# A gated encoder block on one core: four dense units in seven quarter products, results through DRAM, the gMLP output branch beside the last head

## The chip, the cores and the metric

One core of a Trainium2 chip runs the whole kernel in one launch. Its engines work side by side, each through its own list of instructions in order: TensorE (PE, matrix products into the accumulators of PSUM), VectorE (DVE), ScalarE (ACT), GpSimd (POOL) and SyncE (SP, which only issues DMAs here). DMAs are issued by SP and POOL. The metric is the device time of one execution in microseconds (us), the median of the runs shown. The profile is of one further execution of the same program.

## What is computed

One block with batch 1, 1024 tokens and width 1024, cut to what matters here:

```python
h = rmsnorm(x, norm_g) * (1 + scale(c)) + shift(c)
q, k, v, z_gla, ra_f, ra_b, u, vs, z_gmlp, m_gla, m_gmlp = split(h @ w_in)
# GLA: 4 heads, two directions, chunks of 64 tokens, then a norm per head
y_gla  = (norm(gla_fw(q, k, v, ra_f) + gla_bw(q, k, v, ra_b)) * silu(z_gla)) @ w_br_gla
# gMLP: chunks of 128 tokens, 8 groups of 128 features
vs     = layernorm(gelu(vs)) * ln_g + ln_b
sg     = einsum('gts,bnsgc->bntgc', gmlp_ws, vs) + gmlp_bs
y_gmlp = (gelu(u) * sg * silu(z_gmlp)) @ w_br_gmlp
merged = sigmoid(m_gla) * y_gla + sigmoid(m_gmlp) * y_gmlp
out    = rmsnorm(x + gate(c) * (merged @ w_out), final_g)
```

u, z_gmlp, m_gla and m_gmlp are four products of the same h (1024 x 1024) with a 1024 x 1024 weight each. They are the "dense units that share activations".

## The kernel before, in words

**Operands.** Every large product is made of three matmuls. An operand is split into a high part (ACT rounds it to fp32r: `split_w`, L123) and a low part (DVE subtracts: L124), and the product is high x high, high x low, low x high (L140 to L142). h is kept as `H_hi` and `H_lo`, eight tiles each of [128 features, 1024 tokens], in 16 slots of pool `hp`. A weight block of 128 output features is [128, 1024], 512 KB, loaded by SP into `ws` (L117), split into `wh` and `wl`.

**`dense_fm`** (L133) makes one block of 128 output features over all tokens: for each half of the tokens it accumulates 8 chunks x 3 matmuls of 512 columns in one accumulator (three of these, tag `d`, rotate) and hands it to an `evac` function.

**Order of the work.** The startup builds h and with it the first column half of vs; then the second half (`evac_vs1`, L393), each tile followed by `ln` (L382: gelu, statistics, scaling, and a pass each for the gain `lng` and the bias `lnb`), the spatial products (L399 to L408, `sg` kept in SBUF), then stage M2 (L420 to L443): eight times a block of u and a block of z_gmlp, and their product split into `gg_hi`, `gg_lo`. Stage M3 (L446 to L485) builds the residual gate (eight loads `wg`, L459, sums on DVE, two matmuls) and takes eight times a block of m_gmlp, tanh, and a block of the gMLP output branch (`FB_YB`), whose result goes to DRAM as `y2_d` (L482, issued by POOL). Then GLA: `dense_q`, `dense_v0`, `dense_k`, `dense_z` for head 0; in the loop over heads (L774) the dense blocks of head h+1 stand beside the chain of head h (`front`, `body`), which is given a high priority; beside heads 2 and 3 stand the eight blocks of m_gla (`dense_ma`, L740). A head's result goes to `g_d` in DRAM (L736). At the end all heads' results are loaded and split (L792 to L803), the GLA output branch (`ev_ya`, L818) merges both branches, and the projection with `w_out` (L883 to L899) ends with the residual and the final norm.

**Who sets the order.** The instructions are written as a program; a planner then orders each engine's list. It takes what is ready by its own estimate of time, earlier written lines first, unless a priority, `keep_in_program_order` or `issue_after` says otherwise. A tile waits for the last use of the slot that it takes. A pool that is opened where another lay waits tile by tile for what lies under it.

Of the kernel before, what the change touches and what calls it, by code (L numbers as in the profile page):

```python
# [37 lines left out]
PC_C, PC_NG, PC_BA, PC_GN = 0, 8, 16, 32  # L38
# packed rows
PR_FG, PR_LG, PR_LB, PR_BG, PR_BS, PR_C = 0, 1, 2, 3, 4, 5  # L40
# [3 lines left out]
def hybrid_block_kernel(ctx: ExitStack, tc: tile.TileContext, x, wf, wt, wada, wgate, wvr, wst, alpha, abias,  # L44
# [18 lines left out]
    cw, wp = pool("wp")  # L63
    dr = ctx.enter_context(tc.tile_pool(name="dr", bufs=1, space=DRAM))
    y2_d = dr.tile([KC, P, T], F32, tag="y2d", name="y2_d")
    g_d = dr.tile([KC - 2, P, T], F32, tag="gd", name="g_d")
# [32 lines left out]
    pcol = cp.tile([P, 40], F32, name="pcol")  # L99
    RT = cp.tile([P, T], F32R, name="RT")  # L100
# [6 lines left out]
    H_hi = [None] * KC  # L107
    H_lo = [None] * KC
    for k in range(KC):
        H_hi[k] = hp.tile([P, T], F32R, tag="h", bufs=16, name=f"hhi{k}")  # L110
        H_lo[k] = hp.tile([P, T], F32R, tag="h", bufs=16, name=f"hlo{k}")

    pin = [True]

    def stage(src):
        w = wp.tile([P, 1024], F32, tag="ws", bufs=2, name=nm("ws"))
# [8 lines left out]

    def fm_weights(b):
        w = stage(wf[b])
        hi = wp.tile([P, KC, P], F32R, tag="wh", bufs=2, name=nm("wh"))
        lo = wp.tile([P, KC, P], F32R, tag="wl", bufs=2, name=nm("wl"))
        split_w(w, hi.rearrange("p k c -> p (k c)"), lo.rearrange("p k c -> p (k c)"))  # L130
        return hi, lo

    def dense_fm(b, xh, xl, evac):  # L133
        """out^T block b (128 features) over all tokens; evac(half, psum)"""
        hi, lo = fm_weights(b)
        for half in range(2):
            acc = pd()
            sl = slice(half * 512, half * 512 + 512)
            for k in range(KC):
                TE.matmul(acc, lhsT=hi[:, k, :], rhs=xh[k][:, sl], start=(k == 0), stop=False)  # L140
                TE.matmul(acc, lhsT=hi[:, k, :], rhs=xl[k][:, sl], start=False, stop=False)  # L141
                TE.matmul(acc, lhsT=lo[:, k, :], rhs=xh[k][:, sl], start=False, stop=(k == KC - 1))  # L142
            evac(half, acc)

    def tm_weights(w0, p_, tag, bufs, prep=None):
        pieces = []
        for j in range(4):
# [3 lines left out]
            hi = p_.tile([P, 2, 512], F32R, tag=tag, bufs=bufs, name=nm("th"))  # L151
            lo = p_.tile([P, 2, 512], F32R, tag=tag, bufs=bufs, name=nm("tl"))
            split_w(w, hi.rearrange("p k c -> p (k c)"), lo.rearrange("p k c -> p (k c)"))
# [3 lines left out]
    def tm_step(acc, pieces, xh, xl, k, t):  # L157
        hi, lo = pieces[k // 2]
        tsl = slice(t * P, t * P + P)
        TE.matmul(acc, lhsT=xh[k][:, tsl], rhs=hi[:, k % 2, :], start=(k == 0), stop=False)  # L160
        TE.matmul(acc, lhsT=xh[k][:, tsl], rhs=lo[:, k % 2, :], start=False, stop=False)  # L161
        return TE.matmul(acc, lhsT=xl[k][:, tsl], rhs=hi[:, k % 2, :], start=False, stop=(k == KC - 1))  # L162

    def dense_tm(pieces, xh, xl, evac, tokens=range(NT)):
        for t in tokens:
            acc = pd()
            for k in range(KC):
# [802 lines left out]
```

## Time and profile before

| | us |
|---|---|
| median of 3 runs | 1119.02 |
| lowest, highest | 1118.24, 1119.49 |
| span of the profiled execution | 1115.8 |
| PE busy in it | 1093.1 |
| DVE, ACT, POOL busy | 567.9, 425.9, 109.7 |

The span runs from the first to the last instruction; the profiled execution has no other time of its own, and what lies around the span (launch and end) is only in the runs' times. A line of the profile's groups gives line, engine and operation, result and operands by the program's names, shapes, count, then busy time in us and mean ns of one, then the engine's idle time just before them and what ended it. The windows view gives, for each stretch of time, its length, PE's busy time with the count of matmuls, the granted clock and the DMA's share and rate. In the timeline a row begins with its start and its duration in us.

### The profile page before, as it was taken

The numbers are of one execution on the slowest core, as the hardware profiler recorded it, in microseconds if no ns is written. First come the engines' busy times: TensorE is split into PE (matmuls) and PEld (weight loads), VectorE is DVE, ScalarE is ACT, GpSimd is POOL, SyncE is SP. The second block draws the span as 40 slices with busy tenths as digits, with TensorE's granted clock in tenths as the row PEclk, the third lists the DMA queues.
The fourth block names the chain that finished last, engine by engine and source line by source line (L and its number), as shares of the span: only waits on it lengthen the run. The fifth ranks groups of instructions, "written<-read, shape, count | busy, mean of one in ns | idle before, by whom it ended". The sixth has DMA issues, their size and how long they took to land.

```text
span 1115.8 us, 13854 instructions
## 1 busy us (share of the span) xinstructions
PE 1093.1 (98%) x5584; PEld 932.1 (84%) x5584; DVE 567.9 (51%) x982; ACT 425.9 (38%) x768; POOL 109.7 (10%) x136
## 2 busy tenths in 40 slices
PE   6899999999999999999999999999999999999996
PEld 4788888888888888889898898899888888888885
DVE  6868753333344111111456787786677534555232
ACT  4452112222221111112565776777576424222232
POOL 3320100000010000000000010000000013013520
PEclk9999999999999999999999999999999999999999
DMA  8632011111153121211020030020111135213412
GB/s 315 251 125 71 1 39 38 57 39 56 54 171 127 64 76 66 82 66 57 22 75 19 22 111 19 20 95 20 58 38 57 38 108 194 76 58 124 160 76 95
DMA packets 25650, 90.39 MB, mean 81 GB/s; under 512 B 3471, under 2 KB 3471, under 8 KB 25586
## 3 DMA queue, kind: packets, MB, share of 16 engines
q1 hardware_dynamic: 18866, 67.27, 17.2%
q0 software_dynamic: 6720, 22.23, 5.8%
q8 instruction: 44, 0.72, 0.3%
q14 instruction: 20, 0.16, 0.0%
HBM read 77.96 MB, written 11.53 MB: 80 GB/s over the span
## 4 chain that ended last, share of the span: by engine, by line
PE 94%; DVE 2%; DMA 1%; ACT 1%; issue 1%; POOL 0%; SPq 0%; POOLq 0%; ACTq 0%
PE pd L140 21%; PE pd L142 21%; PE pd L141 21%; PE pd L161 4%; PE pd L162 4%; PE pd L160 4%; PE pd L765 2%; PE pd L764 2%; PE pd L763 2%; PE pm L404 1%; PE pm L604 1%; PE po L630 1%; PE po L628 1%; PE po L629 1%; PE pd L546 1%; PE pd L547 1%
## 5 line engine op out<-in xcount | busy, mean ns | idle before, releaser
L140 PE MATMUL pd<-hhi,wh 128*128 128x512 f32 x768 | 300.4, 391 | 0.0
L142 PE MATMUL pd<-hhi,wl 128*128 128x512 f32 x768 | 300.4, 391 | 0.0
L141 PE MATMUL pd<-hlo,wh 128*128 128x512 f32 x768 | 300.4, 391 | 0.0
L142 PEld LDWEIGHTS pd<-hhi,wl 128*128 128x128 f32 x768 | 144.3, 188 | 28.9 <-issue 0.2
L140 PEld LDWEIGHTS pd<-hhi,wh 128*128 128x128 f32 x768 | 144.3, 188 | 28.5 <-issue 0.2
L141 PEld LDWEIGHTS pd<-hlo,wh 128*128 128x128 f32 x768 | 144.3, 188 | 28.0
L124 DVE TENSOR_TENSOR wl<-ws,wh 128x1024 fp32r<-128x1024 f32 x64 | 78.1, 1222 | 149.5 <-ACT wh L123 139.4
L123 ACT CAST wh<-ws 128x1024 fp32r<-128x1024 f32 x64 | 67.3, 1051 | 221.2 <-PE pd L141 209.2
L176 POOL TENSOR_TENSOR r<-ms,nhalf 128x1 f32<-128x1 f32 (+1 forms) x24 | 20.6, 859 | 427.9 <-DVE ms L175 422.5
L765 PE MATMUL pd<-tvh,hlo 128*128 128x256 f32 x192 | 54.5, 284 | 0.0
L764 PE MATMUL pd<-tvl,hhi 128*128 128x256 f32 x192 | 54.4, 283 | 0.0
L763 PE MATMUL pd<-tvh,hhi 128*128 128x256 f32 x192 | 54.3, 284 | 0.0
L141 PE MATMUL pd<-ggl,wh 128*128 128x512 f32 x128 | 49.8, 389 | 0.0
L142 PE MATMUL pd<-ggh,wl 128*128 128x512 f32 x128 | 49.8, 389 | 0.0
L141 PE MATMUL pd<-gl,wh 128*128 128x512 f32 x128 | 49.8, 389 | 0.0
L140 PE MATMUL pd<-ggh,wh 128*128 128x512 f32 x128 | 49.8, 389 | 0.0
L142 PE MATMUL pd<-gh,wl 128*128 128x512 f32 x128 | 49.6, 389 | 0.0
L140 PE MATMUL pd<-gh,wh 128*128 128x512 f32 x128 | 48.8, 390 | 0.0
L161 PE MATMUL pd<-tl,mh 128*128 128x512 f32 x120 | 46.8, 390 | 0.4 <-DVE tl L124 0.4
L162 PE MATMUL pd<-th,ml 128*128 128x512 f32 x120 | 46.7, 389 | 0.0
L160 PE MATMUL pd<-th,mh 128*128 128x512 f32 x120 | 45.6, 389 | 0.0
L160 PE MATMUL pd<-th,hhi 128*128 128x512 f32 x104 | 41.6, 404 | 1.2 <-ACT hhi L276 1.2
(246 smaller groups left out, 1986.9 us busy)
## 6 DMA issues: line engine op xcount, KB each, us to landing
ws<-in_wf SPq DMA_DIRECT2D x64, 512.0 KB, 3.5
ws<-in_wt SPq DMA_DIRECT2D x22, 512.0 KB, 3.7
wa<-in_wada SPq DMA_DIRECT2D x16, 512.0 KB, 4.7
xn<-in_x SPq DMA_DIRECT2D x8, 512.0 KB, 5.5
wg<-in_wgate POOLq DMA_DIRECT2D x8, 512.0 KB, 4.2
y_d<-m POOLq DMA_DIRECT2D x16, 256.0 KB, 2.3
y<-y_d POOLq DMA_DIRECT2D x16, 256.0 KB, 4.6
res<-in_x SPq DMA_DIRECT2D x8, 512.0 KB, 6.4
```

Source lines behind the costliest of these rows:

```text
L123: S.copy(hi, w)
L124: V.tensor_tensor(out=lo, in0=w, in1=hi.bitcast(F32), op=ALU.subtract)
L140: TE.matmul(acc, lhsT=hi[:, k, :], rhs=xh[k][:, sl], start=(k == 0), stop=False)
L141: TE.matmul(acc, lhsT=hi[:, k, :], rhs=xl[k][:, sl], start=False, stop=False)
L142: TE.matmul(acc, lhsT=lo[:, k, :], rhs=xh[k][:, sl], start=False, stop=(k == KC - 1))
L160: TE.matmul(acc, lhsT=xh[k][:, tsl], rhs=hi[:, k % 2, :], start=(k == 0), stop=False)
L161: TE.matmul(acc, lhsT=xh[k][:, tsl], rhs=lo[:, k % 2, :], start=False, stop=False)
L162: return TE.matmul(acc, lhsT=xl[k][:, tsl], rhs=hi[:, k % 2, :], start=False, stop=(k == KC - 1))
L176: G.tensor_tensor(out=r, in0=ms, in1=nhalf[:, 0:n], op=ALU.pow)
L763: TE.matmul(o, lhsT=H_hi[k][:, tsl], rhs=hi, start=(k == 0), stop=False)
L764: TE.matmul(o, lhsT=H_hi[k][:, tsl], rhs=lo, start=False, stop=False)
L765: TE.matmul(o, lhsT=H_lo[k][:, tsl], rhs=hi, start=False, stop=(k == KC - 1))
```

## The change

**Seven products.** h and a pair of weight blocks are taken as 2 x 2 quarters: h by feature half and token half (B11, B12, B21, B22), the pair by block and feature half. Instead of eight quarter products (four results, two each), seven are formed, of sums and differences of the quarters (Strassen's scheme in Winograd's form). T1 to T4 are such sums of h, made once on POOL, split, and kept for all sixteen pairs; the sums of the weights are made on POOL for each pair. Three accumulators X, Y, Z are used, with parts in between added by DVE.

**Memory.** h is now tiles of [128, two chunks, 512 tokens] (`Act`), one pool of 30 slots (`ht`) holds h, the sums, x, vs and later all of GLA's tiles. h's quarter B12 is not needed by the products, is written to DRAM (`b12_d`) and read back after the pairs.

**Through DRAM.** `sg`, the gated product `gg`, tanh of m_gla (`ta`) and of m_gmlp (`tb`) are written to DRAM and read where they are used.

**Order.** vs takes tiles 4 to 7, then their spatial products, then tiles 0 to 3 and theirs; the layernorm's gain and bias are applied behind the spatial product. The residual gate is built before the pairs, with one buffer for its loads. The gMLP output branch (`dense_yb`) stands beside head 3, where m_gla was, with `gg` reloaded into h's slots.

The core of the diff:

```diff
+    def ht(shape, dtype, name):
+        return hp.tile(shape, dtype, tag="h", bufs=30, name=nm(name))
...
-        V.tensor_scalar(vs[t], vs[t], mv[:, 0:1], r, op0=ALU.subtract, op1=ALU.mult)
-        V.tensor_tensor(out=vs[t], in0=vs[t], in1=lng, op=ALU.mult)
-        V.tensor_tensor(out=vs[t], in0=vs[t], in1=lnb, op=ALU.add)
+        V.tensor_scalar(vs[t], vs[t], mv[:, 0:1], r, op0=ALU.subtract, op1=ALU.mult)
...
+    def spatial(half):
+        for g in range(8):
+            pg = pm()
...
+            sg = Mp.tile([P, 4, P], F32, tag="sg", bufs=2, name=nm("sg"))
+            V.scalar_tensor_tensor(out=sg, in0=pg.rearrange("p (n t) -> p n t", t=P),
+                                   scalar=pcol[:, PC_LG + g:PC_LG + g + 1],
+                                   in1=bsb[:, g:g + 1, :].broadcast_to([P, 4, P]), op0=ALU.mult, op1=ALU.add)
+            G.dma_start(sg_d[g, :, half * 512:half * 512 + 512], sg.rearrange("p n t -> p (n t)"))
+
+    for b in range(2):
+        pw = pm()
+        TE.matmul(pw, lhsT=ones, rhs=wsT[:, 4 * b:4 * b + 4, :].rearrange("p g t -> p (g t)"), start=True, stop=True)
...
+    for t in range(4, 8):
+        vs1(t)
+    spatial(1)
+    for t in range(4):
+        vs1(t)
+    spatial(0)
+
+    TS = [Act(f"t{i}") for i in range(4)]
+    for c in range(2):
+        def whole(cc_, half):
+            r = ht([P, 2, 512], F32, "r")
+            G.tensor_tensor(out=r, in0=H.h[cc_][half].bitcast(F32), in1=H.l[cc_][half].bitcast(F32), op=ALU.add)
+            return r
+
+        def part(i, r):
+            hi, lo = TS[i].make(c, 0)
+            split_w(flat(r), flat(hi), flat(lo))
+
+        r12, r11 = whole(c, 1), whole(c, 0)
+        G.tensor_tensor(out=r11, in0=r12, in1=r11, op=ALU.subtract)
+        r22 = whole(c + 2, 1)
+        G.tensor_tensor(out=r12, in0=r22, in1=r12, op=ALU.subtract)
+        G.tensor_tensor(out=r22, in0=r22, in1=r11, op=ALU.subtract)
+        part(1, r22)
+        part(2, r12)
+        part(0, r11)
+        r21 = whole(c + 2, 0)
+        G.tensor_tensor(out=r21, in0=r21, in1=r22, op=ALU.subtract)
+        part(3, r21)
...
+    for k in range(KC):
+        wg = Mp.tile([P, D], F32, tag="wg", bufs=1, name=nm("wg"))
+        G.dma_start(wg, wgate[k])
...
+    bg = Mp.tile([P, D], F32, tag="wg", bufs=1, name="bg")
...
+    cW, Wp = pool("W", side="right")
+
+    def prod(acc, wh, wl, xh, xl, first):
+        for k in range(4):
+            a, b = wh[:, k * P:(k + 1) * P], wl[:, k * P:(k + 1) * P]
+            TE.matmul(acc, lhsT=a, rhs=xh(k), start=(first and k == 0), stop=False, skip_group_check=not first)
+            TE.matmul(acc, lhsT=a, rhs=xl(k), start=False, stop=False, skip_group_check=not first)
+            TE.matmul(acc, lhsT=b, rhs=xh(k), start=False, stop=(k == 3), skip_group_check=not first)
...
+    def wt_(tag, n):
+        return [Wp.tile([P, n], F32R, tag=tag + x, bufs=1, name=nm(tag + x)) for x in "hl"]
...
+    def pair(ba, bb, evac):
+        wa = Wp.tile([P, 1024], F32, tag="wa", bufs=2, name=nm("wa"))
+        wb = Wp.tile([P, 1024], F32, tag="wb", bufs=2, name=nm("wb"))
+        nc.sync.dma_start(wa, wf[ba])
+        nc.sync.dma_start(wb, wf[bb])
+        L, R = slice(0, 512), slice(512, 1024)
+        ws = Wp.tile([P, 1024], F32, tag="wsum", bufs=1, name=nm("wsum"))
+        G.tensor_tensor(out=ws[:, L], in0=wb[:, L], in1=wb[:, R], op=ALU.add)
+        G.tensor_tensor(out=ws[:, R], in0=ws[:, L], in1=wa[:, L], op=ALU.subtract)
+        G.tensor_tensor(out=wb[:, L], in0=wa[:, L], in1=wb[:, L], op=ALU.subtract)
+        ah, al = wt_("a", 1024)
+        split_w(wa, ah, al)
+        sh, sl = wt_("s", 1024)
+        split_w(ws, sh, sl)
+        G.tensor_tensor(out=wa[:, R], in0=wa[:, R], in1=ws[:, R], op=ALU.subtract)
+        bh, bl = wt_("b", 1024)
+        split_w(wb, bh, bl)
+        fh, fl = wt_("f", 512)
+        split_w(wa[:, R], fh, fl)
+        X = pd()
+        prod(X, ah[:, L], al[:, L], *B11, True)
+        p1 = tmp("p1")
+        S.copy(p1, X)
+        Y = po_()
+        prod(Y, sh[:, R], sl[:, R], *T2, True)
+        u2 = tmp("u2")
+        V.tensor_tensor(out=u2, in0=Y, in1=p1, op=ALU.add)
+        prod(X, ah[:, R], al[:, R], *B21, False)
+        evac(0, 0, X)
+        prod(Y, bh[:, L], bl[:, L], *T3, False)
+        u3 = tmp("u3")
+        V.tensor_tensor(out=u3, in0=Y, in1=p1, op=ALU.add)
+        Z = pk_()
+        prod(Z, sh[:, L], sl[:, L], *T1, True)
+        V.tensor_tensor(out=u3, in0=Z, in1=u3, op=ALU.add)
+        evac(1, 1, u3)
+        prod(Y, bh[:, R], bl[:, R], *T4, False)
+        V.tensor_tensor(out=p1, in0=Y, in1=p1, op=ALU.add)
+        evac(1, 0, p1)
+        prod(Z, fh, fl, *B22, False)
+        V.tensor_tensor(out=u2, in0=Z, in1=u2, op=ALU.add)
+        evac(0, 1, u2)
...
+    pair_m(FB_MB, tb_d, 0)
+    pair_m(FB_MB, tb_d, 1)
+    pair_uz(0)
...
+    pair_m(FB_MA, ta_d, 0)
+    pair_uz(3)
+    for i in range(1, 4):
+        pair_m(FB_MA, ta_d, i)
+    close(cW)
+
+    for c in range(2):
+        hi, lo = H.make(c, 1)
+        nc.sync.dma_start(flat(hi).bitcast(F32), b12_d[2 * c])
+        nc.sync.dma_start(flat(lo).bitcast(F32), b12_d[2 * c + 1])
...
+    def load_gg():
+        for half in range(2):
+            for c in range(KC // 2):
+                hi, lo = GG.make(c, half)
+                g = vt([P, 2, 512], F32, "ggf")
+                for i in range(2):
+                    nc.sync.dma_start(g[:, i, :], gg_d[2 * c + i, :, half * 512:half * 512 + 512])
+                split_w(flat(g), flat(hi), flat(lo))
...
-        for j in ([], [], [0, 1, 2], [3, 4, 5, 6, 7])[h]:
-            dense_ma(j)
+        else:
+            load_gg()
+            for j in range(KC):
+                dense_yb(j)
```

`pair_m` ends each quarter with tanh (ACT) into a tile `m` of four buffers and a store issued by POOL. `pair_uz` makes a pair of u (gelu into `ht` tiles) and a pair of z_gmlp, whose ending has tanh, three DVE operations, a load of `sg` and a store of `gg`, both issued by POOL ("z pair" below). After the pairs GLA's weight tiles (`wp`) are opened, and `vt` is `ht`.

More of the change, by code (lines that the diff above doesn't have):

```diff
@@ L180, in hybrid_block_kernel @@
     cX, Xp = pool("X", side="right")
+    wpool[0] = Xp
     def xt(shape, dtype, name):
-        return Xp.tile(shape, dtype, tag="x", bufs=18, name=nm(name))
+        return Xp.tile(shape, dtype, tag="x", bufs=8, name=nm(name))
     cS, Sp = pool("S")
-    ones = Sp.tile([P, P], F32, name="ones")
-    V.memset(ones, 1.0)
     crow = xt([P, D], F32, "crow")[0:1, :]
-    xn = [xt([P, D], F32, "xn") for _ in range(NT)]
+    xn = [ht([P, D], F32, "xn") for _ in range(NT)]
     def fetch_x(t):
@@ L275, in make_h @@
             S.activation(h32, pt, AF.Identity, bias=ab[:, 0:1], scale=ab[:, 1:2])
[L276 to L277 removed]
+            act = S.copy(hh, h32)
+            V.tensor_tensor(out=hl, in0=h32, in1=hh.bitcast(F32), op=ALU.subtract)
         return act
[L280 removed]
+    vs_w = [(ht([P, 2, 512], F32R, "th"), xt([P, 2, 512], F32R, "tl")) for _ in range(4)]
     vs_s = {}
@@ L472, in hybrid_block_kernel @@
     V.tensor_scalar(gate, gate, 0.5, None, op0=ALU.mult)
[L473 to L485 removed]
+    close(cM)
@@ new lines, in pair_m, with ev, pair_uz, ev_u @@
+    def pair_m(b0, d, i):
+        def ev(b, half, acc):
+            m = Wp.tile([P, 512], F32, tag="z", bufs=4, name=nm("m"))
+            S.activation(m, acc, AF.Tanh, scale=0.5)
+            G.dma_start(d[2 * i + b, :, half * 512:half * 512 + 512], m)
+        pair(b0 + 2 * i, b0 + 2 * i + 1, ev)
+    def pair_uz(i):
+        u = [ht([P, T], F32, "u") for _ in range(2)]
+        def ev_u(b, half, acc):
+            S.activation(u[b][:, half * 512:half * 512 + 512], acc, AF.Gelu)
+        def ev_z(b, half, acc):
+            sl = slice(half * 512, half * 512 + 512)
+            sg = Wp.tile([P, 512], F32, tag="sg", bufs=3, name=nm("sgl"))
+            G.dma_start(sg, sg_d[2 * i + b, :, sl])
+            z = Wp.tile([P, 512], F32, tag="z", bufs=4, name=nm("z"))
+            S.activation(z, acc, AF.Tanh, scale=0.5)
+            V.scalar_tensor_tensor(out=z, in0=z, scalar=1.0, in1=acc, op0=ALU.add, op1=ALU.mult)
+            uu = u[b][:, sl]
+            V.tensor_tensor(out=uu, in0=uu, in1=sg, op=ALU.mult)
+            V.scalar_tensor_tensor(out=uu, in0=uu, scalar=0.5, in1=z, op0=ALU.mult, op1=ALU.mult)
+            G.dma_start(gg_d[2 * i + b, :, sl], uu)
+        pair(FB_U + 2 * i, FB_U + 2 * i + 1, ev_u)
+        pair(FB_ZG + 2 * i, FB_ZG + 2 * i + 1, ev_z)
@@ L772, in hybrid_block_kernel, with dense_yb, ev @@
     dense_z(0)
+    GG = Act("gg")
+    def load_gg():
+        for half in range(2):
+            for c in range(KC // 2):
+                hi, lo = GG.make(c, half)
[3 more added lines that the diff above has]
+                split_w(flat(g), flat(hi), flat(lo))
+    def dense_yb(j):
+        tb, y = vt([P, T], F32, "tb"), vt([P, T], F32, "yb")
+        def ev(half, acc):
+            sl = slice(half * 512, half * 512 + 512)
+            nc.sync.dma_start(tb[:, sl], tb_d[j, :, sl])
+            V.scalar_tensor_tensor(out=y[:, sl], in0=tb[:, sl], scalar=1.0, in1=acc, op0=ALU.add, op1=ALU.mult)
+            G.dma_start(y2_d[j, :, sl], y[:, sl])
+        dense_fm(FB_YB + j, GG, ev)
     for h in range(HEADS):
```

271 lines of the change are left out of this document (130 added, 141 removed).

## The prediction, made before the changed kernel was run

> **What bounds the kernel now.** I read the page first: busy shares, the slices, then the chain that ended last.
>
> ```profile
> span 1115.8 us, 13854 instructions
> PE 1093.1 (98%) x5584; PEld 932.1 (84%) x5584; DVE 567.9 (51%) x982; ACT 425.9 (38%) x768; POOL 109.7 (10%) x136
> PE   6899999999999999999999999999999999999996
> PEclk9999999999999999999999999999999999999999
> PE 94%; DVE 2%; DMA 1%; ACT 1%; issue 1%; POOL 0%; SPq 0%; POOLq 0%; ACTq 0%
> L140 PE MATMUL pd<-hhi,wh 128*128 128x512 f32 x768 | 300.4, 391 | 0.0
> ```
>
> PE is busy in every slice but the first and last, and 94% of the chain is PE. A busy share can hide gaps, since a matmul counts 391 ns from start to modelled end while its successor is already running. So I took the windows view over stretches that hold only 512-column matmuls and divided time by count.
>
> ```profile
> core 0: us, PE busy (x), PEclk, DMA share, GB/s
> 350.00:480.00 130.00, 130.00 (x575) 1.00 0.21 73
> 960.00:1012.00 52.00, 52.00 (x232) 1.00 0.15 51
> ```
>
> 130/575 is 226.1 ns for one matmul in the stage that the change rewrites, and 52/232 is 224.1 ns in the GLA output branch, the same rate within 1%. Two stages with different neighbours agree, so there the rate is PE's own, not that of waits. Between the startup and the last projection a matmul removed is 0.226 us removed, and a PE wait added is added in full.
>
> **The products.** Before, each of 32 blocks (u, z_gmlp, m_gla, m_gmlp, eight each) takes 2 halves x 8 chunks x 3 = 48 matmuls, 1536 in all. After, each of 16 pairs takes 7 products x 4 chunks x 3 = 84 of the same shape, 1344. 192 fewer x 226.1 ns = **-43.4 us**, and a pair takes 84 x 226.1 ns = 19.0 us, a product 2.71 us. The Trainium skill (TensorE: Matmul & The Clock Gate, Part 1) gives 215.7 ns between warm matmuls of 512 columns; by it the saving would be 41.4 us. The trace's own rate is used.
>
> **Added PE work.** The layernorm's gain and bias move behind the spatial product: `ones` x `wsT`, two fp32 matmuls of 512 columns. Their like in the trace is the gate's pair, four instructions, from the chain by time:
>
> ```profile
> 344.08 1.72 PE pm L469 x4
> 147.63 7.61 PE pm L404 x64
> ```
>
> So **+1.7 us**. The spatial matmuls keep their count (7.6 us a half). The branch's eight blocks move, unchanged, to where m_gla's eight were.
>
> **The pair loop.** The other engines' rows, by line and shape, and the DMA issues:
>
> ```profile
> L124 DVE TENSOR_TENSOR wl<-ws,wh 128x1024 fp32r<-128x1024 f32 x64 | 78.1, 1222 | 149.5 <-ACT wh L123 139.4 <-PE po L556 9.5
> L433 DVE SCALAR_TENSOR_TENSOR z<-z,pd 128x512 f32<-128x512 f32 x16 | 10.9, 683 | 23.4 <-ACT z L432 23.4
> L123 ACT CAST wh<-ws 128x1024 fp32r<-128x1024 f32 x64 | 67.3, 1051 | 221.2 <-PE pd L141 209.2 <-DMA ws<-in_wf 6.9 <-PE pd L142 3.5
> L385 DVE BATCH_NORM_STATS2 st<-vs 128x6 f32<-128x512 f32 x16 | 10.8, 682 | 5.3 <-ACT vs L352 5.2
> L432 ACT ACTIVATE z<-pd 128x512 f32<-128x512 f32 x16 | 9.5, 593 | 44.1 <-PE pd L142 28.5 <-DVE sg L406 15.6
> L856 POOL TENSOR_TENSOR res<-res,fg 128x512 f32<-128x512 f32 x8 | 11.3, 1417 | 11.2 <-ACT jk L853 11.2
> L290 POOL TENSOR_TENSOR tl<-ws,th 128x1024 fp32r<-128x1024 f32 x4 | 11.2, 2796 | 5.7 <-ACT th L289 5.7
> L482 POOL DMA_DIRECT2D y_d<-m x16 | 8.7, 541 | 144.5 <-DVE m L481 144.4
> ws<-in_wf SPq DMA_DIRECT2D x64, 512.0 KB, 3.5
> y_d<-m POOLq DMA_DIRECT2D x16, 256.0 KB, 2.3
> wg<-in_wgate POOLq DMA_DIRECT2D x8, 512.0 KB, 4.2
> gt<-g_d POOLq DMA_DIRECT2D x12, 256.0 KB, 4.1
> ```
>
> Per pair of 19.0 us: DVE has 3.5 weight splits (4.3 us), 5 adds from PSUM at 0.68 (3.4) and, in the four z pairs, 12 gate operations (8.2): 7.7 us, or 15.9. ACT: 3.5 casts (3.7), one copy and four functions at 0.59: 6.7 us. POOL: four half-tile sums (5.7), and at most 8 DMA issues at 0.54 (4.3): 10 us. All fit under 19.0, the z pairs' DVE at 84%.
>
> PE waits only where an accumulator is reused: X after the copy to `p1`, Y after `u2` and again after `u3`, Z after its add. Each reader has one product, 2.71 us, as cover and needs 0.6 to 0.7 us. Weights `a`, `s`, `b`, `f` are single-buffered: `s` is free after product 5 of seven and needed by the next product 2, three products or 8.1 us later, for a cast and a subtract of 2.3 us; the others have four products or more. Loads of 3.5 us come a pair ahead. Cost in the loop: at least 0; at most one DVE operation in front of one reuse in each z pair and its follower, 8 x 1.22 = 10 us. I take **2**, near the lower end, as 0.7 against 2.71 is.
>
> **The four joints** are where PE could stand still. Stage ends, from timelines of ACT, POOL and DVE:
>
> ```profile
> 77.81 0.48 DVE L272 SCALAR_TENSOR_TENSOR hlo<-h,ab,hhi 128x256 fp32r<-128x256 f32 x1 [0.19 <-ACT hhi L271]
> 79.94 0.52 POOL L378 DMA_DIRECT2D sa<-in_alpha  x1 [16.85 <-DVE sa L376]
> 92.00 1.04 ACT L410 CAST sr<-sa 128x1024 fp32r<-128x1024 f32 x1
> 118.71 0.60 ACT L352 ACTIVATE vs<-pd 128x512 f32<-128x512 f32 x1 [4.84 <-PE pd L162]
> 124.15 0.60 ACT L352 ACTIVATE vs<-pd 128x512 f32<-128x512 f32 x1 [4.84 <-PE pd L162]
> 324.34 1.28 DVE L463 SCALAR_TENSOR_TENSOR gacc<-wg,gsc,gacc 128x1024 f32<-128x1024 f32 x1 [1.48 <-DMA wg<-in_wgate]
> 341.82 1.28 DVE L463 SCALAR_TENSOR_TENSOR gacc<-wg,gsc,gacc 128x1024 f32<-128x1024 f32 x1 [1.57 <-DMA wg<-in_wgate]
> 822.98 0.59 ACT L513 ACTIVATE zg<-pd 128x512 f32<-128x512 f32 x1
> 838.19 0.54 POOL L736 DMA_DIRECT2D g_d<-zg  x1 [0.39 <-DVE zg L733]
> ```
>
> *Front.* vs ends at 124.2 now. After, half the spatial products and the bias lie between the vs tiles, so vs ends near 124.2 + 7.6 + 1.7 = 133.5, and without a wait pair 0 could start 7.6 us later, at 141. Then u's matmuls no longer stand by as filling, as they do now. PE waits for the last layernorm (gelu 0.59, two statistics at 0.68, a scaling about as long, POOL's power), about 4 us, then the spatial half: its `sg` has two buffers and each is stored before reuse, 0.7 + 0.54 + 2.3 = 3.5 us for two, so eight take 14 us where PE needs 7.6; the first pair's products, with weights there 3.5 + 2.3 us after vs, can lie in between. They need the sums T1 to T4: 16 POOL operations of 2.8 us, 45 us, possible from 78.3 (the last h) on, with tile slots short until the first spatial half is done. And pair 0 writes tiles that lie on the gate's `wg` and `gacc` (tile sizes in the code, per partition: 131 KB of constants and `h` slots, 28 KB for stage M1, 74 KB for W from the other side, 233 KB together, where the largest stage of before adds up to 207 KB; so I take it that they overlap), so the gate must be done: nine loads on one buffer. With two buffers six steps took 341.82 - 324.34 = 17.5 us, 2.9 each, so 5.8 us on one, 52 us, from about 84: done near 136, later by what POOL's queue makes them wait (45 us of sums between). Bounds 0 and 12 us; **5**, the layernorm's wait and a little.
>
> *Pairs to GLA.* The new weight tiles lie where the last pair's `m` tiles were. After the last product: add 0.7, tanh 0.6, issue 0.5, store 2.3, cast 1.05, subtract 1.2: 6.4 us at most; nothing if v of head 0 goes ahead of q, for which room is free. **3**.
>
> *H to the gate product.* The 16 tiles of the product take h's slots, which fall free with z of head 3 (now 822.98). Eight reloads, casts and subtracts, 8 x 1.22 = 9.8 us of DVE, meet head 2's end (838.19), whose chain goes first. Bounds: 0, as half of it is free one half-block (5.4 us) early and POOL's and SP's queues are light; above, 9.8 plus a load (4.1, as of `gt`) = 14. **3**, nearer to the lower end since PE has head 2's own matmuls meanwhile.
>
> *Last branch and projection*: the same tiles and waits, one load more per half, issued from SP; 0.
>
> None can go below nothing: PE's slices show no gap at these places now, and what is taken off DVE (two layernorm passes a tile) was off the path.
>
> Sum: 1115.8 - 43.4 + 1.7 + 2 + 5 + 3 + 3 = **1087.1 us** of span. The runs' median lies 1119.0 - 1115.8 = 3.2 us above the span (launch and end); so **1090.3 us**. About 0.2% (2.2 us) is what a measurement of this kernel can tell from no change.
>
> **Rivals.**
> *POOL's queue holds the first pair (slower).* POOL works in order. If its instructions stand as written, the T sums (45 us) follow the second spatial half's stores (about 147) and the gate's loads (52 us) follow them: pair 0 goes on at 244 instead of 141 + 5 = 146, +98 us, about 1188. It turns slower once the gate ends later than 146 + 29 = 175. Against it: the planner orders by readiness. L410, written behind the spatial products, ran at 92.00, amid vs. Chance 0.07.
> *Hand-offs in the pairs.* If adds come late behind other DVE work, each of 4 x 16 reuses slips. At 3.1 us of latency instead of 0.7 it loses 0.4 x 64 = 26 us in place of the 2: 1114. For it, DVE's 84% in z pairs; against, twelve of sixteen pairs at 41%. Chance 0.07.
> *The clock drops at the joints.*
>
> ```profile
> 0.00:50.00 50.00, 36.72 (x148) 0.97 0.80 297
> 1100.00:1116.00 16.00, 6.73 (x53) 0.85 0.23 88
> ```
>
> Where PE stands still the granted clock falls: 0.97 with 13 us idle, 0.85 with 9 idle, that is 1.5 and 2.4 us lost. At four joints up to 2.4 us more each: 1090.3 + 9.6 = 1100. The Trainium skill (TensorE: Matmul & The Clock Gate, Part 1) says that an idle window of about 3.4 us halves the clock until as long a busy one; these two rows agree in kind. For it: the front's 4 us wait. Chance 0.07.
> *The change doesn't do what it says*: the planner spreads the products so that nothing is won; about 1119. Chance 0.02.
>
> **Numbers.** Forecast 0.77. Joints and loop at nothing give 1077.3; front and H joint at their upper ends give 1090.3 + 7 + 11 = 1108.3. The range 1077 to 1109 takes in the clock case and leaves out part of the hand-off case, the slower one and the one of no change. Faster 0.77 + 0.07 + 0.07 = 0.91, same 0.02, slower 0.07.
>
> **What would show it.** 1344 matmuls of the pair lines at 226 ns; the first pair's start near 146 and the last one's end near 146 + 16 x 19.0 + 2 = 452; PE gaps at these four places and their releasers: layernorm, `sg` store, `wg`, the `m` store, the split of the reloaded product. A pair that takes over 20 us of PE time, or a start after 175, makes the prediction wrong.

## The result, and the profile after

The change makes the kernel slower. The median of four runs is 1151.8 us (1149.67 to 1154.03), against 1118.63 us for the kernel before, measured beside it: a ratio of 1.0295, with an interval from 1.0273 to 1.0316. The forecast was 1090.3 us, and "slower" had a chance of 0.07. The profiled execution took 1149.67 us, and its span is 1148.0 us, 32.2 us longer than before. In every run whose span is on record the execution takes 1.6 to 1.9 us more than its span.

The page of the kernel after, with the lines that answer to those shown of before:

```profile
span 1148.0 us, 14156 instructions
PE 1080.8 (94%) x5396; PEld 907.8 (79%) x5396; DVE 667.0 (58%) x1079; ACT 467.6 (41%) x810; POOL 268.0 (23%) x270
PE   6999855999999999989999999999989999999997
POOL 3216487343434343200000010000000110012420
PEclk9899867999999999999999999999999999999999
PE 83%; DVE 6%; DMA 4%; ACT 3%; issue 3%; POOL 1%; SPq 0%; POOLq 0%; DVEq 0%; ACTq 0%
```

The matmuls did go away, yet PE's busy time fell only from 1093.1 to 1080.8 us. The slices say where to look: one is 28.7 us long, and slices 5 to 7 (about 115 to 200 us) read 8, 5, 5 for PE, 8, 6, 7 for its clock and 4, 8, 7 for POOL. DVE, ACT and DMAs are now on the chain.

Some events stand in both kernels and can be laid side by side: the first tile of vs's second half leaves PSUM, q of head 0 leaves it, head 2's last store goes out (its row of before is in the prediction), the GLA output branch begins. The timeline rows of before, then those of after:

```profile
86.07 0.60 ACT L352 ACTIVATE vs<-pd 128x512 f32<-128x512 f32 x1 [1.80 <-PE pd L162]
500.16 0.59 ACT L496 ACTIVATE q<-pd 128x512 f32<-128x512 f32 x1
931.36 0.39 PE L140 MATMUL pd<-gh,wh 128*128 128x512 f32 x1
```

```profile
90.32 0.60 ACT L380 ACTIVATE vs<-pd 128x512 f32<-128x512 f32 x1 [0.31 <-PE pd L200]
512.77 0.60 ACT L643 ACTIVATE q<-pd 128x512 f32<-128x512 f32 x1 [6.63 <-PE pd L182]
855.43 0.60 POOL L883 DMA_DIRECT2D g_d<-zg  x1 [6.92 <-DVE zg L880]
957.41 0.39 PE L180 MATMUL pd<-gh,wh 128*128 128x512 f32 x1
```

The lag behind the kernel before is thus 4.3 us at vs, 12.6 at q, 17.2 at head 2's last store (838.19 before), 26.1 at the output branch and 32.2 at the end. Between vs and q lie the front and the pairs, where 43.4 us of matmuls were taken out: that stretch should have gained 43.4 us and lost 8.3 instead, so 51.7 us were added in it. Behind q another 19.6 us were added, in three portions of 4.6, 8.8 and 6.2. The last of them has two parts, as the issue of the last store shows, before and then after:

```profile
1109.82 0.38 SPq L877 DMA_DIRECT2D out_y<-res  x1
```

```profile
1144.52 0.38 SPq L1034 DMA_DIRECT2D out_y<-res  x1
```

The lag at this store is 34.7 us, so the branch and the projection took some 8.7 us more. From there to the span's end it takes 6.0 us before and 3.5 after: the closing of the kernel after is 2.5 us shorter.

The windows view tells which part of the stretch. The columns are the busy times of PE, PEld, DVE, ACT and POOL with counts, then granted clock, DMA share and GB/s:

```profile
100.00:150.00 50.00, 42.14 (x199) 34.35 (x197) 44.16 (x54) 7.67 (x10) 24.73 (x26) 0.93 0.27 91
150.00:200.00 50.00, 26.42 (x92) 19.60 (x93) 28.05 (x24) 8.22 (x9) 37.94 (x29) 0.64 0.38 137
300.00:350.00 50.00, 50.00 (x220) 41.05 (x219) 28.53 (x35) 17.02 (x24) 22.19 (x22) 1.00 0.28 100
```

The pairs run as forecast (300 to 350 us: PE without a gap). The loss is the front: from 150 to 200 us PE holds matmuls for 26.42 of 50 us at a clock of 0.64. PE's waits there, from its timeline:

```profile
157.89 4.44 PE L436 MATMUL pm<-wsT,vs 128*128 128x128 f32 x18 [6.36 <-DVE vs L423]
166.33 3.78 PE L436 MATMUL pm<-wsT,vs 128*128 128x128 f32 x16 [4.00 <-DVE sg L439]
180.98 3.42 PE L513 MATMUL pm<-gacc,ones 128*128 128x512 f32 x4 [4.93 <-DVE sg L439]
187.29 0.78 PE L527 MATMUL pd<-hh,ah 128*128 128x512 f32 x1 [2.88 <-ACT ah L161]
195.00 0.80 PE L527 MATMUL po<-t1h,sh 128*128 128x512 f32 x1 [2.89 <-ACT sh L161]
```

The first pair starts at 187.29 instead of the 146 of the forecast. PE waits for a layernorm scaling, for the gate product's `sg`, then for the weights. These are DVE rows, and DVE itself was held up. Its timeline and POOL's, after:

```profile
97.65 6.86 DVE L486 CAST ST<-sr 64x1024 fp32r<-64x1024 f32 x1
113.76 5.91 DVE L423 TENSOR_SCALAR vs<-vs,mv,r 128x1024 f32<-128x1024 f32 x2
165.52 1.41 DVE L439 SCALAR_TENSOR_TENSOR sg<-pm,pcol,bsb 128x512 f32<-128x512 f32 x2 [6.05 <-DMA sg_d<-sg]
170.60 0.75 DVE L439 SCALAR_TENSOR_TENSOR sg<-pm,pcol,bsb 128x512 f32<-128x512 f32 x1 [3.66 <-DMA sg_d<-sg]
```

```profile
93.39 7.07 POOL L465 TENSOR_TENSOR r<-hh,hl 128x1024 f32<-128x1024 f32 x3
101.56 2.40 POOL L473 TENSOR_TENSOR r<-r,r 128x1024 f32<-128x1024 f32 x1
112.72 3.35 POOL L475 TENSOR_TENSOR r<-r,r 128x1024 f32<-128x1024 f32 x1
```

and the same two operations before:

```profile
93.99 0.63 DVE L411 CAST ST<-sr 64x1024 fp32r<-64x1024 f32 x1
105.65 0.81 DVE L389 TENSOR_SCALAR vs<-vs,mv,r 128x1024 f32<-128x1024 f32 x1
```

A cast of 0.63 us took 6.86 and ended at 104.51, just behind POOL's sum of 101.56 to 103.96; two scalings of 0.81 each took 5.91 together, the first ending at 116.62, just behind the sum that ended at 116.07, and the second at 119.67, behind the next one:

```profile
116.76 2.35 POOL L476 TENSOR_TENSOR r<-r,r 128x1024 f32<-128x1024 f32 x1
```

From 85 to 190 us seven rows of DVE are longer than the shortest of their kind (the cast: than in the kernel before), together by 17.5 us. Each of the seven overlaps a sum on POOL, and the kernel before has no such row in this stretch. Two more things show: `sg` waits for its own stores, and the weights come after the last `sg` (layout: the first weight tiles lie on stage M1's).

### The profile page after: what moved, and what is told of

It reads as the page before. It is cut to its first block, busy times and chain, and to the rows that moved or that the text cites. A ratio compares the mean times of both kernels' runs of the same rounds, so it can differ in the third digit from the quotient of the medians.

```text
span 1148.0 us, 14156 instructions
## 1 busy us (share of the span) xinstructions
PE 1080.8 (94%) x5396; PEld 907.8 (79%) x5396; DVE 667.0 (58%) x1079; ACT 467.6 (41%) x810; POOL 268.0 (23%) x270
## 4 chain that ended last, share of the span: by engine, by line
PE 83%; DVE 6%; DMA 4%; ACT 3%; issue 3%; POOL 1%; SPq 0%; POOLq 0%; DVEq 0%; ACTq 0%
PE pd L182 10%; PE pd L180 10%; PE pd L181 9%; PE po L527 4%; PE po L528 4%; PE po L529 4%; PE pd L199 4%; PE pd L200 4%; PE pd L198 3%; PE pk L528 3%; PE pk L527 3%; PE pk L529 3%; PE pd L528 2%; PE pd L527 2%; PE pd L529 2%
## 5 line engine op out<-in xcount | busy, mean ns | idle before, releaser
L180 PE MATMUL pd<-hh,wh 128*128 128x512 f32 x256 | 100.7, 393 | 2.4 <-ACT wh L161 2.4
L181 PE MATMUL pd<-hl,wh 128*128 128x512 f32 x256 | 100.4, 392 | 0.0
L182 PE MATMUL pd<-hh,wl 128*128 128x512 f32 x256 | 100.1, 392 | 0.1
L180 PEld LDWEIGHTS pd<-hh,wh 128*128 128x128 f32 x256 | 48.1, 188 | 11.8 <-ACT wh L161 2.9
L902 PE MATMUL pd<-tvh,hl 128*128 128x256 f32 x192 | 54.5, 284 | 0.0
L901 PE MATMUL pd<-tvl,hh 128*128 128x256 f32 x192 | 54.3, 283 | 0.0
L900 PE MATMUL pd<-tvh,hh 128*128 128x256 f32 x192 | 54.3, 283 | 0.0
L527 PE MATMUL pd<-hh,ah 128*128 128x512 f32 x128 | 50.9, 398 | 2.9 <-ACT ah L161 2.9
L528 PE MATMUL pd<-hl,ah 128*128 128x512 f32 x128 | 50.9, 397 | 0.0
L529 PE MATMUL pd<-hh,al 128*128 128x512 f32 x128 | 50.4, 394 | 0.1
```

Of the source, the lines that this page charges most:

```text
L180: TE.matmul(acc, lhsT=hi[:, k, :], rhs=x.hi(k, half), start=(k == 0), stop=False)
L181: TE.matmul(acc, lhsT=hi[:, k, :], rhs=x.lo(k, half), start=False, stop=False)
L182: TE.matmul(acc, lhsT=lo[:, k, :], rhs=x.hi(k, half), start=False, stop=(k == KC - 1))
L527: TE.matmul(acc, lhsT=a, rhs=xh(k), start=(first and k == 0), stop=False, skip_group_check=not first)
L528: TE.matmul(acc, lhsT=a, rhs=xl(k), start=False, stop=False, skip_group_check=not first)
L529: TE.matmul(acc, lhsT=b, rhs=xh(k), start=False, stop=(k == 3), skip_group_check=not first)
```

## The experiments

Five theories for the front were tried, and two further questions. **A**: POOL's sums shut DVE out. **B**: the `sg` stores and their two buffers. **C**: the first weights lie on tiles that are read late. **E**: DVE has too much to do there. **F**: PE has nothing to fill the front with. Beside each time stands where the last pair's last product ends in the profile (503.8 us in the kernel after), since from there to the end it took 639 to 656 us in these runs, although few of the edits touch that part. In the kernels with the stores by SP and with the weights elsewhere (both below), PE, ACT, DVE and POOL do the work behind the pairs in the very order of the kernel after, so there the order is not the reason. Part of the difference is slower matmuls behind the joints (with the stores by SP the granted clock is 0.91 in the 20 us around q, from 491 to 511, where the kernel after has 1.00 from 500 to 520); another part stands at the very end. Of POOL's closing instructions one, a drain, takes 2.2 us in the kernel after and 10.1 in the kernel with the stores by SP (the third of the three times, in ns, is the longest):

```profile
L1130 POOLq DRAIN  x3: 46/93/2217, 1142.7 to 1147.7; - x3
```

```profile
L1130 POOLq DRAIN  x3: 46/93/10057, 1138.8 to 1149.7; - x3
```

From the last store's issue to the span's end it takes 3.3 to 3.5 us in the changed kernels that issue the `sg` stores from POOL, and 7.8 to 9.4 in those that issue them from SP. Why is open. This closing stands behind all of the work, but it is in every total below.

**One suspect at a time.** The sums on DVE:

```diff
-            G.tensor_tensor(out=r, in0=H.h[cc_][half].bitcast(F32), in1=H.l[cc_][half].bitcast(F32), op=ALU.add)
+            V.tensor_tensor(out=r, in0=H.h[cc_][half].bitcast(F32), in1=H.l[cc_][half].bitcast(F32), op=ALU.add)
...
-        G.tensor_tensor(out=r11, in0=r12, in1=r11, op=ALU.subtract)
+        V.tensor_tensor(out=r11, in0=r12, in1=r11, op=ALU.subtract)
```

(and the three other differences alike.)

> The 16 sums that make T1 to T4 of h run on DVE instead of POOL; nothing else changes. Theory A (POOL's sums hold the front: while one runs, DVE's operations with two inputs from SBUF or in their fast form wait, and the sg stores and gate loads queue behind it): the delayed DVE rows (L486 6.9 us, L423 5.9 us for two) fall to their usual 0.6 and 0.8 us, the second spatial half takes about 14 us instead of 25, the first pair starts near 160 instead of 187, time about 1125. Theory B (two sg buffers and the landing of each store set the pace): first pair near 182, time about 1147. Theory C (the first weights can only be loaded when the spatial half is over, because of where the tiles lie): first pair 3 us after the last sg as now, time 1140 or more.

Measured: 1146.36 us, ratio 1.0263 (1.0244 to 1.0283); last pair's end 500.5. The first pair starts at 176.43, 10.9 us earlier, and reaches its last matmul at 203.2 instead of 219.6; DVE's scalings take their 0.8 us again. But the order of the products in a pair came out differently, and each pair waits once:

```profile
244.55 0.50 PE L527 MATMUL pk<-t0h,sh 128*128 128x512 f32 x1 [0.55 <-DVE u L584]
```

A pair takes 20.07 us instead of 19.23, 14 x 0.84 = 11.8 us, most of what the front gained. So A shows in the front, and the time hides it.

The stores by SP:

```diff
-            G.dma_start(sg_d[g, :, half * 512:half * 512 + 512], sg.rearrange("p n t -> p (n t)"))
+            nc.sync.dma_start(sg_d[g, :, half * 512:half * 512 + 512], sg.rearrange("p n t -> p (n t)"))
```

> The 16 stores of sg are issued by SP instead of POOL, so they no longer queue behind POOL's sums; the sums stay on POOL. Theory A: the spatial half gets shorter by the queueing part alone, about 10 of the 25 us, while DVE's delayed rows stay; time about 1141. Theory B (the stores' landing with two buffers): no change beyond 2 us, 1150. Theory C: the pair starts as much earlier as the last sg does, and its first products still wait for loads.

Measured: 1149.83 us, 1.0284 (1.0264 to 1.0304): by these intervals the same as the kernel after. But the pairs end 9.3 us earlier (494.5), and the first pair is as much ahead, so stores that queue behind POOL's sums do cost the front some 9 us, as A's expectation had it. The rest of the kernel takes 11.3 us longer, 5.9 of them behind the last store.

The weights elsewhere:

```diff
     cW, Wp = pool("W", side="right")
+    cWz, Wz = pool("Wz", side="right")
+    cWv, Wv = pool("Wv", side="right")
+    cWu, Wu = pool("Wu", side="right")
+    cWs, Ws = pool("Ws", side="right")
```

with the small output tiles taken from these.

> The pair stage's tiles are put into five pools in another order, so that its weight tiles lie above all tiles of the stage before and the short-lived ones (sums u2, u3, p1, endings, sg) below; nothing else changes. Theory C: the first weights load right after vs (about 146), product 1 and 2 of the first pair fill PE's waits in the spatial half, and the wait for the second operand's sum (now 3 us, 191.7 to 195.0) goes; time about 1137. Theory A: the sums T2 are late anyway, so little is won, about 1147.

Measured: 1146.66 us, 1.0264 (1.024 to 1.0288); last pair's end 498.9. The first product now comes at 148.01, but the later ones still wait for `sg` and for the sums, so 39 us at the first product became 4.9 at the last.

**Is it PE that paces the pairs?** The first product of each pair done twice:

```diff
         prod(X, ah[:, L], al[:, L], *B11, True)
+        prod(X, ah[:, L], al[:, L], *B11, True)
```

> Each pair computes its first product twice (the second overwrites the first), so eight quarter products' worth of matmuls, 192 more; the result is the same. If a removed matmul was worth the 226.1 ns of the window, this costs 192 x 0.226 = 43.4 us over the changed kernel: about 1195. If the pairs had slack on PE (another engine setting their pace), less: 1152 to 1175.

Measured: 1190.63 us, 1.0657 (1.0641 to 1.0673): 38.8 us more than the kernel after for 192 matmuls, 202 ns each, where one takes 229 ns in the pairs (19.23 us for 84). In the middle of the stage a pair takes 21.97 us on average, 228 ns for each of its twelve added matmuls; the total is lower because the first pair, with more to do while it waits, ends 2.7 us earlier in spite of them. PE paces the pairs, so the 192 matmuls that the change removed were worth about their price.

**The three suspects together** (the three edits above, `sg` with four buffers, and Z in the two accumulators that the front is done with), then the same with the sums left on POOL, then all edits and the squares' junk output put elsewhere:

```diff
-            sg = Mp.tile([P, 4, P], F32, tag="sg", bufs=2, name=nm("sg"))
+            sg = Mp.tile([P, 4, P], F32, tag="sg", bufs=4, name=nm("sg"))
...
-        Z = pk_()
+        Z = pm()
```

> All three suspects of the front at once: the quarter sums run on VectorE, the gate product's stores are issued by SP out of four buffers instead of two, and the first pair's weight tiles lie above tiles that are read late no longer; and the seventh product's accumulator Z takes the two banks that the front has done with, so that a pair needs not wait for the last reading of the pair before it (0.55 us a pair where the sums ran on VectorE). If the front's loss is these three (A, B and C), the first pair's product starts near 160 instead of 187.29 and the time falls by some 27 us, to 1122 to 1128. If the front is bound by the chain from the last product over the layernorm and the gate product to the first pair whatever the buffers are (rival), the first pair starts no earlier than 172 and the time stays above 1135.

> The kernel with all edits of the front but one: the quarter sums stay on GpSimd. If GpSimd's sums cost by shutting VectorE out (A), VectorE's casts and scalings beside them still take 3 to 7 us each where they took 0.6 to 0.8, and the time is 8 to 12 us above the kernel with all edits. If the price came only from the stores that stood in GpSimd's queue behind the sums (B), which SP issues here, the two kernels agree within 3 us.

> The kernel with all edits of the front, and the junk output of the squares at the projection written to the accumulator instead of to a tile of the shared slots. If the 4.9 us at the projection's second half come from slots of the shared 30 that free late, the wait of 2.52 us for a weight piece near the end goes and the time is 3 to 5 us under the kernel with the front's edits alone. If they come from where the order puts the loads, nothing changes (within 1 us).

Measured: 1136.51 us, 1.0187 (1.0154 to 1.022) with all edits; 1155.44 us, 1.0338 (1.032 to 1.0356) with the sums left on POOL. The engine of the sums alone makes 18.9 us between the two (14.5 at the last pair's end, 499.6 against 485.1). With POOL's sums in place, the other edits bring 4.2 us at the last pair's end, fewer than the stores by SP alone, and nothing in time. In that kernel, DVE's row and then POOL's:

```profile
152.29 6.23 DVE L162 TENSOR_TENSOR t3l<-r,t3h 128x1024 fp32r<-128x1024 f32 x1
```

```profile
150.49 6.95 POOL L465 TENSOR_TENSOR r<-hh,hl 128x1024 f32<-128x1024 f32 x3
```

and DVE's like in the kernel with the sums on DVE:

```profile
108.71 1.22 DVE L162 TENSOR_TENSOR t1l<-r,t1h 128x1024 fp32r<-128x1024 f32 x1
```

The subtract took 6.23 us instead of 1.22: it ended at 158.52, 1.1 us (about its own length) after POOL's three sums ended at 157.44. The Trainium skill (SBUF — State Buffer, "SBUF: two separate sides") says that GpSimd and a VectorE operation in a two-port mode or with two SBUF inputs take a shared port pair as an exclusive lock for a whole instruction. These rows agree, and add that sums standing back to back let the waiting operation in only when all three were done.

In the kernel with the sums on DVE, no DVE row ahead of the first pair is stretched. So A holds. All three together gave 15.3 us of time where 27 were expected, and 18.7 at the last pair's end (5.6 us went behind the last store). So the front is held by more than A, B and C. The squares' edit,

```diff
-        jk = ht([P, 512], F32, "jk")
+        jk = acc
```

gave 1134.36 us, 1.0149 (1.0129 to 1.0169). The wait of 2.52 us near the end of the projection is gone; the difference of 2.2 us in time lies within the intervals.

**What holds the front then?** The first weights on tiles that are free early, and the layernorm's scaling on ACT; and the same without the gate's chain:

```diff
+    cWa, Wa = pool("Wa", side="right")
     cW, Wp = pool("W", side="right")
...
-        V.tensor_scalar(vs[t], vs[t], mv[:, 0:1], r, op0=ALU.subtract, op1=ALU.mult)
+        S.activation(vs[t], vs[t], AF.Identity, bias=nb, scale=r)
```

> The kernel with the front's edits and the squares' edit, and two more: the first pairs' weight tiles lie on top of tiles that are free once the vs weights are split (in the kernel with the front's edits their first load still went out at 168.5, after the last gate product, and ScalarE sat 7.54 us on it), and the layernorm's scaling runs on ScalarE. If the layout of the first weights is what still holds the front (theory C in its full form), the first pair's first product starts before 160 instead of 173.5, and the time falls by 10 to 16 us, to 1118 to 1125. If VectorE's own work in the front (sums, splits, gate chain: 45 of 50 us busy from 100 to 150) is the bound (theory E), TensorE has the first product early but then waits for the sums' parts, and no more than 5 us come back.

> The same kernel, and the output gate's chain left out (its eight loads, its eight steps on VectorE and its four fp32 products; the gate is set to a constant, so a part of the computation is missing). What it saves beside the kernel with the gate is the price of having the gate's chain in the front: under theory E (VectorE is the bound there) about its eight steps, 10 us, and the four products' 2 to 4 us on top; under theory C about the four products alone, 2 to 4 us.

Measured: 1134.22 us, 1.0132 (1.0104 to 1.016), with the first product at 149.16 instead of 173.53: 24 us earlier, and the time is the same (the pairs end at 481.1 instead of 484.9). So C is not what bounds the front. Without the gate 1125.06 us, 1.0061 (1.0039 to 1.0083), 9.2 us less (7.2 at the pairs' end), for about 10 us of DVE steps and four products on PE. The windows of 150 to 200 us, with the gate, then without:

```profile
150.00:200.00 50.00, 42.06 (x183) 32.45 (x183) 38.33 (x41) 14.87 (x19) 23.03 (x19) 0.88 0.35 129
```

```profile
150.00:200.00 50.00, 42.99 (x196) 34.01 (x195) 32.02 (x33) 17.53 (x22) 22.02 (x20) 0.91 0.36 127
```

So E for the gate's chain: with POOL out of the way, DVE's own work is on the front's path. Not all of it is, as the next runs show.

**The gate moved into the pairs**, in full; then the low-rank gates' weights moved too; then the gate alone in the kernel after:

```diff
+    def gate_step(k):
+        for b in range(2):
+            sl = slice(b * 512, b * 512 + 512)
+            wg = Wz.tile([P, 512], F32, tag="z", bufs=4, name=nm("wg"))
+            nc.sync.dma_start(wg, wgate[k, :, sl])
...
     pair_m(FB_MB, tb_d, 1)
+    gate_step(0)
+    gate_step(1)
     pair_uz(0)
```

> The kernel with the first weights on top, whose gate chain moves out of the front into the stage of the pairs (sixteen half loads by SP into the slots of the pairs' small outputs, the steps on VectorE between the pairs, the four fp32 products near the end of that stage): nothing is left out. Under theory E (VectorE's work in the front is the bound) the 9 us that leaving the gate out saved come back but for the four products' 2 us: 1126 to 1129. If what the gate cost were its loads or its work as such, wherever it stands, nothing changes: 1133 to 1136.

> The same, and the low-rank gates' weights (loads, six steps on VectorE of 4.6 us together, one cast on ScalarE) moved from the front to the first product of the GLA stage. Under theory E another 3 to 5 us: 1121 to 1125, which is 3 to 7 us slower than the kernel before. If VectorE is no longer the bound in the front once the gate has left, no change beside the run before it (within 1.5 us).

> The kernel after the change, with the gate chain alone moved from the front into the stage of the pairs. If VectorE's load by itself is the bound in the front (E), some 8 to 10 us come back: 1142 to 1144. If it is held there by GpSimd's sums (A), which this leaves in place, the gate's steps only fill time that VectorE would spend shut out, and no more than 4 us come back: 1148 or more.

None of the three brought time. 1135.44 us, 1.0153 (1.0139 to 1.0167): the first pair reached its last matmul 5.7 us earlier (191.79 against 197.46), as E has it, but the pairs lost 8.8 us: a pair took 19.60 us instead of 19.23, also where no gate step lies, and the gate's last products with a wait took 3.4. With the low-rank weights moved, 1144.7 us, 1.0223 (1.0201 to 1.0244): no gain in the front (the first pair's last matmul at 195.91), so these 4.6 us of DVE were not on its path, and behind the pairs 656.3 us instead of 648.7, with PE waiting 2.43 us at 506.71 for v's weights `tvh`, which came behind the moved work. In the kernel after, 1153.72 us, 1.0316 (1.0302 to 1.033): no gain in time, as A expected. But the first pair reached its last matmul 6.8 us earlier (212.8 instead of 219.6), which is more than the 4 that A allowed; the slower pairs (19.60 us) and the gate's end took it back, so this run does not decide between A and E.

> The kernel with all edits of the front and the gate's chain among the pairs, with the gate's last products and additions put behind the last pair, where TensorE waits 6 us for the GLA stage's first weights anyway, and with the new small constant tile 64 bytes long instead of 32, so that no tile behind it is shifted by half a step. If the 8.8 us that the pairs lost were the gate's end (3.4) and addresses (5.2 by the slower pitch), both come back and the time is 1126 to 1129, 8 to 11 us slower than the kernel before. If the pitch has another cause, a pair still takes 19.60 us and the time stays at 1131 to 1134.

```diff
-    gsc = cp.tile([P, 8], F32, name="gsc")
+    gsc = cp.tile([P, 16], F32, name="gsc")[:, 0:8]
...
+    gate_end()
```

Measured: 1135.12 us, 1.0151 (1.0135 to 1.0166). The gate's end came back (the pairs end 4.0 us earlier, at 480.2), though not in the time. A pair still took 19.52 us: the shift by half a step is not the cause, and what slowed the matmuls by 1.5% in the four kernels with the gate among the pairs stays open.

**Does want of filling cost the front?** The first pair of blocks, then the first two, in the old eight products, which need h alone:

```diff
-    pair_m(FB_MB, tb_d, 0)
+    pair_m(FB_MB, tb_d, 0, pair8)
```

> The kernel with all edits of the front (sums on VectorE, first weights on top, layernorm's scaling on ScalarE; gate in the front), whose first pair of blocks is made in the old eight products of h alone, so that 96 matmuls (22 us) need no sum. If the front loses time for want of products that need only h (theory F), TensorE fills some 15 us of its waits with them and the time falls by 5 to 15 us, to 1119 to 1129, although twelve matmuls (2.7 us) more are done. If VectorE's queue is the bound whatever TensorE does meanwhile, the work behind it only moves: 1134 to 1140.

> The same with the first two pairs in eight products: under theory F the first pair has filled most of the front, so the second gives little or costs up to its 2.7 us; the time lies within 4 us of the run with one such pair. If VectorE's queue is the bound, it adds 2.7 us at least.

Measured: 1126.08 us, 1.0068 (1.0045 to 1.0091), 8.1 us under the kernel with all edits of the front though it does twelve matmuls more; with two, 1130.32 us, 1.0115 (1.01 to 1.0131). F holds, and one pair fills what can be filled: the second costs 4.2 us, a little more than its matmuls and than was expected. From 150 to 200 us:

```profile
150.00:200.00 50.00, 48.89 (x229) 39.62 (x228) 35.69 (x36) 16.30 (x20) 23.32 (x20) 0.97 0.38 137
```

PE 48.89 instead of 42.06, the clock 0.97 instead of 0.88. This is the fastest full version with the seven products, and it is still 8.7 us slower than the kernel before (1117.43 us beside it), 3.1 of them behind the last store.

**The joint to gMLP's product**, left out (the output branch multiplies h instead):

```diff
-            load_gg()
+            pass
...
-        dense_fm(FB_YB + j, GG, ev)
+        dense_fm(FB_YB + j, H, ev)
```

> The kernel after the change, with the reload and the split of gMLP's product left out: the output branch of gMLP multiplies the activations in its place (a part of the computation is missing). If the joint between the activations' last use and the reloaded product costs what its waits and the cold clock behind them show in the trace (8.6 us more than the same stretch before), the time falls by 7 to 10 us, to 1142 to 1145. If the waits only move work that TensorE has to wait for later in any case, it falls by less than 3.

Measured: 1142.24 us, 1.0214 (1.0197 to 1.0231), 9.6 us less. From head 2's last store to the output branch it takes 93.1 us (855.04 to 948.12), as before the change (93.2), instead of 102.0. In the kernel after, PE's rows there:

```profile
847.31 0.50 PE L181 MATMUL pd<-ggl,wh 128*128 128x512 f32 x1 [1.25 <-DVE ggl L162]
850.87 0.50 PE L180 MATMUL pd<-ggh,wh 128*128 128x512 f32 x1 [1.76 <-ACT ggh L161]
870.34 0.50 PE L181 MATMUL pd<-ggl,wh 128*128 128x512 f32 x1 [1.00 <-DVE ggl L162]
872.86 0.50 PE L180 MATMUL pd<-ggh,wh 128*128 128x512 f32 x1 [0.81 <-DVE yb L928]
```

## Why the prediction was wrong

**Right.** The products' worth: doubling one cost 202 ns a matmul over the whole kernel and 228 in the middle of the pairs, of a stated 226, and from 300 to 350 us 220 matmuls took 50 us. The pair loop: a pair takes 19.23 us instead of 19.0, 16 x 0.24 = 3.9 us, for which "2" with bounds 0 and 10 was given. The size is near by luck: the 2 stood for waits at the reuse of an accumulator, and none waits there; the matmuls themselves come 0.229 us apart instead of 0.226. The bias products: four matmuls between 94.5 and 96.4 us, about the 1.7. Pairs to GLA: q comes 9.0 us behind the last product (503.77 to 512.77), and 24 matmuls take 5.4 of it and the last one's end 0.2, so 3.4 for "3".

**The step that failed** is the front: "Bounds 0 and 12 us; 5, the layernorm's wait and a little". Of the 51.7 us added between vs and q, 1.7, 3.9 and 3.4 are accounted for above, so the front took some 43 us. The prediction's sum went through PE and through the DMAs; what it left out was DVE. It listed the sums as POOL's, "16 POOL operations of 2.8 us, 45 us", "possible from 78.3", and asked only when they end, not whom they hold up (the last of them ended at 184.18); and it never added up DVE in the front (8 gate steps, 8 splits, the scalings, the low-rank weights, `sg`). DVE was busy for 44.16 of 50 us from 100 to 150, some 10 of which are the stretch of the rows beside POOL's sums. Of `sg` it had "eight take 14 us"; the second half's eight took 24 (158.72 to 182.63). The runs give the front's parts: 14.5 us at the last pair's end and 18.9 in time for POOL's sums, shown by moving them alone where the front's other edits were in place; 9 us for the stores that queue behind them, shown by moving these; 7 to 9 us for the gate's chain with DVE freed, shown by leaving it out; 8 us net for the missing filling, shown by one pair in eight products. They overlap and need not add up. The clock of 0.64 is part of the same loss: most of the first pair's matmuls came 0.43 us apart until about 201, some 5 us lost in this pair alone, where the rival "the clock drops" had 2.4 a joint. It came back to 0.97 where one pair in eight products kept PE at work, so it follows from the waits.

"What is taken off DVE (two layernorm passes a tile) was off the path" was read from a PE that had filling at that time. It said itself that "u's matmuls no longer stand by as filling", and then did not price it.

**The layout.** The prediction had pair 0 write tiles that lie on the gate's, and did not ask which. They are the first weights, which then wait for M1's last tiles. It mattered little: with the sums on DVE, 24 us earlier for the first product changed nothing in time.

**H to the gate product**, "3" with bounds 0 and 14: measured 8.8, and 9.6 us of time came back without it. The mechanism was right (reloads, casts and subtracts beside head 2's end), and the size was nearer to the upper row than to the lower.

**Last branch and projection**, "the same tiles and waits, one load more per half, issued from SP; 0", was wrong by some 8.7 us, of which the shorter closing hides 2.5. PE's rows at the branch and at the projection, then ACT's at the start of vs's second half, all of the kernel after:

```profile
960.88 0.50 PE L181 MATMUL pd<-gl,wh 128*128 128x512 f32 x1 [0.94 <-DVE gl L162]
966.71 0.73 PE L180 MATMUL pd<-gh,wh 128*128 128x512 f32 x2 [1.70 <-ACT gh L161]
1095.00 1.44 PE L198 MATMUL pd<-th,mh 128*128 128x512 f32 x3 [2.52 <-ACT th L161]
```

```profile
84.55 1.04 ACT L161 CAST th<-ws 128x1024 fp32r<-128x1024 f32 x1 [6.62 <-DMA ws<-in_wt]
```

The branch waits for its reloaded operand, the projection for a weight piece; the latter wait went when the squares' output left the shared slots. Two portions were not in the sum at all: 4.3 us at the start, where the second half's first cast waits 6.62 us for its load, and 4.6 us between q and head 2's end. Neither was tried, and what causes them is open. The 3.2 us from span to time ("launch and end") are too many: the runs show 1.6 to 1.9, and the rest lay between one execution and another.

**The rivals.** "POOL's queue holds the first pair" named the right engine and the wrong mechanism: the gate's last step on DVE was done at 155.1 and its last load was issued at 160.0, but its products waited for `sg` until 180.98. What POOL's queue did hold up were the `sg` stores. "Hand-offs in the pairs" did not come true in the change itself, but did in the kernel with the sums on DVE (20.07 us a pair), where a condition for it was met: the single accumulator Z taken first in the next pair.

Could the scheme win here? No run did. Against the 43.4 us stand, in the best version, what remains of the front, the 8.8 us at gMLP's product, the branch and projection, and 3.1 us of closing; the gate's chain costs there too.

## What to carry to other kernels

Before helper work goes to POOL because POOL is idle, look at what DVE does in the same stretch: here elementwise work on POOL was not free for DVE, and the price was paid by whoever waited for DVE. A saving of matmuls is only worth its rate where PE has work; when a change makes nearly every product depend on new preparation, add up the preparing engines stage by stage and keep one block that needs none of it as filling for the joint. And price an edit at the end of its own stage as well as by the total, since the rest can give back as much, even in the same order and even behind the last store.

## What the runs showed of the hardware

A DVE cast of 0.63 us took 6.86 us, and a subtract of 1.22 took 6.23, beside POOL sums of 2.4 us each standing back to back. POOL's longest closing drain took 2.2 us in the kernel after and 10.1 in the kernel that differs only in that SP issues the `sg` stores. One pair's period was the same to 0.01 us in eleven kernels (19.22 to 19.23) and 19.5 to 19.6 in the four with the gate's loads and steps among the pairs, without any PE gap; the runs do not say why.
